# A hybrid encoder layer: one block pair fewer by seven products, and the activation sums of the down-projection on VectorE

## The chip, the cores and the metric

The kernel runs on one core of one Trainium2 chip. The metric is the device time of one execution in microseconds, as the median of several runs; lower is better. Engines are named as in the profile: PE (TensorE, matmul), ACT (ScalarE), DVE (VectorE), POOL (GpSimd), SP (SyncE, which here only issues DMAs). ACT issues some DMAs too; each engine works through its queue in order.

## The reference

One layer on x (512 tokens x 1024 channels), all in float32: four gated token mixers with a merge, cross-attention, and a gated MLP. The change concerns the MLP alone:

```python
hf = _rms_norm(x, norm_ffn_pre[l])                                  # (512, 1024)
u = _dwconv_causal(hf @ w_up[l], ffn_dw[l]) + ffn_dw_b[l]           # (512, 2 * 2816), width 3
u_g, u_v = jnp.split(u, 2, axis=-1)
yff = (jax.nn.silu(u_g) * u_v) @ w_down[l]                          # (512, 1024)
x = x + _rms_norm(yff, norm_ffn_post[l])
```

## The kernel before

**Products.** A float32 product is made of three passes on PE (`mm3`, matmuls on L244): each operand is split into a high part, a cast by ACT, and a low part, a subtraction by DVE. Weights are split on L201 (ACT) and L202 (DVE), operands of the down-projection on L1653 and L1654. High and low weights have rings of four buffers each (`wh`, `wl`), raw weights a ring of two (`wr`). The activations of the MLP lie in two tiles, `hth` and `htl`.

**The up-projection** runs over 22 blocks j of 128 hidden channels, each with a gate half (j, 0) and a value half (j, 1). A plain product `plain(j, i)` is 24 matmuls of 512 columns. `done` evacuates it: a bias step on ACT (L1678), two taps on DVE (L624), and after the second half a Silu on ACT (L1681) and a product on DVE (L1683) into the tile `qa` of the block's pair, `ns.quart[j // 2]`. So there are eleven pairs, q = 0 to 10.

`seven(j)` makes both halves of a block at once from seven quarter products of 12 matmuls of 256 columns instead of eight. For it POOL forms four sums of the block's weights (L1756 to L1760), and sums of the activations lie in `tokh` and `tokl`; DVE adds up the parts in PSUM, and ACT copies parts to `mu` (L1782, L1788, L1790) that PE waits for before it accumulates on. The blocks 5, 7, ... 19 go by seven, each interleaved with the plain block after it; 0 to 4 and 21 are plain.

**The down-projection** goes by seven products over the eleven pairs in two phases of two jobs per pair. It needs two kinds of sums:

- *of the weights* (`Sums`): for each pair ACT issues two loads of `w_down` into `wp` (L568), four additions follow (L572 to L575, on DVE for the pairs 0 to 2 and 10, on POOL otherwise), and ACT issues two stores to `sums` in DRAM (L579). They are spread over the up-projection. The down jobs load them back as `dw` (L591, issued by SP).
- *of the activations* (`down_sums`): for each pair three additions of 128 x 256 on POOL, L1665 and L1666 into a place `pairs`, L1667 into the pair's `qa`. The places are in the tile `z7` for the pairs 0 and 1, which the last block by seven gives up, and in `tokh` and `tokl` for the others.

Each pair's activations and their sums are then split into a quarter of `hth` and `htl`, which the last up product still reads (the first pair goes to `wr` buffers). One more POOL addition per pair (L1888) follows for the second phase.

**Buffers in common.** The tags `dw0` to `dw3` serve `wp` (the first two), the raw weights `wq` of the blocks by seven (the other two) and the down weights `dw` (all four).

**The order** on each engine is set by a scheduler that places the traced instructions by its own times. `tc.issue_after` only queues an instruction behind another on the same engine. The jobs are run by `run_blocks`, which fetches weights three jobs ahead.

## Time and profile before

| | |
|---|---|
| median of 3 runs | 1049.4 us (1047.03 to 1051.22) |
| profiled execution | 1049.59 us |
| its span | 1047.7 us |
| granted clock of PE, mean | 0.993 |
| PE busy | 1024.8 us (98%) |
| DVE busy | 855.1 us (82%) |
| ACT busy | 534.0 us (51%) |
| POOL busy | 290.7 us (28%) |
| HBM traffic over the span | 161 GB/s |

The profiled execution lies within the runs' spread; the 1.9 us between its time and its span are outside the program's instructions. Times in the lines of the profile are microseconds from the start of the span. A timeline line gives start, length, engine, line, operation, output and inputs, shapes, the number of instructions merged, and in brackets how long the engine was idle before and what it waited for; ACTq and SPq are DMA issues. A line of the list of waits gives who waited for whom, the total, the number of times and the longest. A line of the table of stretches gives the stretch, its length, for PE, PEld (weight load), DVE, ACT and POOL the busy time and in brackets the number of instructions, then the granted clock of PE, the DMA engines' share and GB/s. The chain of waits lists, in order of time, the work that the end of the program hung on. A busy PE is not PE at its peak: two matmuls of 512 columns follow each other at 0.2275 us.

### The profile page before, as it was taken

The page shows a single profiled execution, that of the slowest core. Times are in us where ns is not written, and L with a number is a line of the kernel's source. Part 1 is how long each engine was busy: PE and PEld are TensorE (multiplying, and loading weights), DVE is VectorE, ACT ScalarE, POOL GpSimd, SP SyncE. Part 2 cuts the span into 40 slices and gives each one's busy share as a digit, 9 for nine tenths or more (in the row PEclk, how much of TensorE's full clock was granted, in tenths as well). Part 3 has the DMA queues.
Part 4 walks back from the last instruction along what each step waited for, and adds up shares of the span by engine and source line. Part 5 has one row for each costly group of instructions (what it writes and reads, how often), then busy time and mean ns, then how long its engine had stood idle before and what let it go on. Part 6 is the DMA issues. An engine that isn't in the chain of part 4 may idle for free.

```text
span 1047.7 us, 15194 instructions
## 1 busy us (share of the span) xinstructions
PE 1024.8 (98%) x5477; PEld 883.3 (84%) x5477; DVE 855.1 (82%) x1290; ACT 534.0 (51%) x893; POOL 290.7 (28%) x303
## 2 busy tenths in 40 slices
PE   9999999999999999999999999999999999969997
PEld 7888888888888988888888899898789899848885
DVE  7899998677788668878677898769887887879786
ACT  5322222376565465765535666554455454545662
POOL 4001000100020224332000030166077547696001
PEclk9999999999999999999999999999999999989999
DMA  7954333334444356676368743054776566536562
GB/s 252 307 171 106 101 101 101 91 91 127 135 116 114 94 136 180 173 195 172 122 206 266 222 141 121 22 181 127 235 241 200 182 220 204 180 120 221 195 209 90
DMA packets 194129, 169.41 MB, mean 162 GB/s; under 512 B 25295, under 2 KB 165692, under 8 KB 194053
## 3 DMA queue, kind: packets, MB, share of 16 engines
q1 hardware_dynamic: 185011, 136.69, 44.1%
q10 hardware_dynamic: 6482, 23.21, 6.0%
q0 software_dynamic: 2560, 8.54, 2.6%
q8 instruction: 43, 0.70, 0.3%
q14 instruction: 33, 0.27, 0.1%
HBM read 142.18 MB, written 26.23 MB: 161 GB/s over the span
## 4 chain that ended last, share of the span: by engine, by line
PE 87%; DMA 4%; DVE 4%; POOL 2%; issue 2%; ACT 2%; ACTq 0%; SPq 0%; POOLq 0%; DVEq 0%
PE ps_mm L244 38%; PE ps_av L244 23%; PE ps_tr L244 14%; PE ps_sc L244 9%; PE ps_tr L250 1%; DMA dw<-sums 1%; POOL pairs L1666 1%; DMA sums<-wp 1%; DVE wl L202 1%; DMA ptl<-turned 1%; DMA e<-in_w_in 1%; POOL pairs L1665 1%; PE ps_mm L462 1%; DMA wp<-in_w_down 1%; PE ps_av L462 1%
## 5 line engine op out<-in xcount | busy, mean ns | idle before, releaser
L201 ACT CAST wh<-wr 128x1024 fp32r<-128x1024 f32 (+1 forms) x124 | 129.4, 1046 | 185.6 <-PE ps_mm L244 67.7
L202 DVE TENSOR_TENSOR wl<-wr,wh 128x1024 fp32r<-128x1024 f32 (+1 forms) x124 | 161.9, 1307 | 37.5 <-ACT wh L201 36.9
L244 PE MATMUL ps_mm<-htl,wh 128*128 128x512 f32 (+1 forms) x472 | 173.5, 376 | 0.0
L244 PE MATMUL ps_mm<-hth,wh 128*128 128x512 f32 (+1 forms) x472 | 173.5, 376 | 0.0
L244 PE MATMUL ps_mm<-hth,wl 128*128 128x512 f32 (+1 forms) x472 | 173.2, 375 | 0.0
L244 PEld LDWEIGHTS ps_mm<-hth,wl 128*128 128x128 f32 x472 | 87.0, 188 | 15.8
L244 PEld LDWEIGHTS ps_mm<-hth,wh 128*128 128x128 f32 x472 | 87.0, 188 | 15.3 <-ACT hth L164 0.3
L244 PEld LDWEIGHTS ps_mm<-htl,wh 128*128 128x128 f32 x472 | 87.0, 188 | 15.3
L244 PE MATMUL ps_av<-htl,wh 128*128 128x512 f32 (+1 forms) x264 | 97.7, 370 | 0.0
L244 PE MATMUL ps_av<-hth,wh 128*128 128x512 f32 (+1 forms) x264 | 97.6, 370 | 0.0
L244 PE MATMUL ps_av<-hth,wl 128*128 128x512 f32 (+1 forms) x264 | 97.6, 370 | 0.0
L697 DVE SCALAR_TENSOR_TENSOR y<-y,par,y 128x508 f32<-128x508 f32 (+29 forms) x120 | 82.5, 726 | 0.1
L244 PEld LDWEIGHTS ps_av<-htl,wh 128*128 128x128 f32 x264 | 49.6, 188 | 8.2
L244 PEld LDWEIGHTS ps_av<-hth,wl 128*128 128x128 f32 x264 | 49.6, 188 | 8.0
L244 PEld LDWEIGHTS ps_av<-hth,wh 128*128 128x128 f32 x264 | 49.7, 188 | 7.9
L1654 DVE TENSOR_TENSOR wl<-dw,wh 128x1024 fp32r<-128x1024 f32 x32 | 44.0, 1377 | 7.7 <-ACT wh L1653 7.5
L1653 ACT CAST wh<-dw 128x1024 fp32r<-128x1024 f32 x32 | 33.5, 1050 | 17.8 <-PE ps_tr L244 5.7
L244 PE MATMUL ps_tr<-htl,wh 128*128 128x512 f32 (+1 forms) x112 | 40.6, 363 | 0.0
L244 PE MATMUL ps_tr<-hth,wh 128*128 128x512 f32 (+1 forms) x112 | 40.6, 363 | 0.0
L244 PE MATMUL ps_tr<-hth,wl 128*128 128x512 f32 (+1 forms) x112 | 40.4, 360 | 0.0
L1124 POOL TENSOR_SCALAR fbias<-ck,cq 128x128 f32<-128x128 f32 (+3 forms) x32 | 21.3, 670 | 66.2 <-DVE st L1130 61.1
L811 POOL MEMSET qk<- 64x512 f32 x16 | 8.5, 532 | 90.5 <-PE ps_sc L244 31.8
(558 smaller groups left out, 2770.8 us busy)
## 6 DMA issues: line engine op xcount, KB each, us to landing
wr<-in_w_in SPq DMA_DIRECT2D x38, 512.0 KB
wr<-in_w_gate SPq DMA_DIRECT2D x32, 512.0 KB
wr<-in_w_up SPq DMA_DIRECT2D x28, 512.0 KB
wp<-in_w_down ACTq DMA_DIRECT2D x22, 512.0 KB
sums<-wp ACTq DMA_DIRECT2D x22, 512.0 KB
dw<-sums SPq DMA_DIRECT2D x44, 256.0 KB
wr<-in_w_branch SPq DMA_DIRECT2D x16, 512.0 KB
wq<-in_w_up SPq DMA_DIRECT2D x16, 512.0 KB
```

The source lines that it names most:

```text
L201: last_weights[:] = [order(A.copy(hi, raw[:, :n])).ins, low.tensor_tensor(lo, raw[:, :n], hi.bitcast(F32), ALU.subtract).ins]
L202: low.tensor_tensor(lo, raw[:, :n], hi.bitcast(F32), ALU.subtract).ins]
L244: steps_of[:] = [PE.matmul(ps, lhs, rhs, start=start, stop=stop, skip_group_check=again).ins]
L250: turns.append(PE.transpose(ps, x, ident[:n, :n]).ins)
L462: keep(PE.matmul(banks[c][:, :S // 2], w[p == 1][:, k, c * P:(c + 1) * P], ht[p == 2][:, i * 4 + k, :S // 2], start=(i, p, k) == (0, 0, 0) ...
L697: ins = V.scalar_tensor_tensor(dst[:, s:], src[:, :S - s], pc("conv_dw", k * 4 + j), dst[:, s:], ALU.mult, ALU.add)
L811: G.memset(qk[rows[1 - c], 4 + c].bitcast(F32), 0.0)
L1124: G.tensor_scalar(bias[:, :w], ck[j][:, :w], -1.0, cq[:, qt, head:head + 1], ALU.mult, ALU.add)
L1653: A.copy(hi, x)
L1654: V.tensor_tensor(lo, x, hi.bitcast(F32), ALU.subtract)
L1665: G.tensor_tensor(t[:, 0], x[:, 1], x[:, 3], ALU.add)
L1666: G.tensor_tensor(t[:, 1], x[:, 0], x[:, 1], ALU.subtract)
```

## The change

- The blocks 5 to 17 go by seven (seven pairs of blocks); 19, 20 and 21 are plain.
- `down_sums` runs on DVE instead of POOL. The sums of the pairs 0 and 1 get a place in the tag `qa10` from the start and are traced in the rounds of the blocks 9 and 13; those of the pairs 2 to 5 with the last plain products; those of 6 to 10 inside the down-projection's first phase, two pairs ahead. Places for the pairs 2 to 10 are taken once the last block by seven is through, two blocks of plain products earlier than before. The last pair's `qa` moves into `tokl`.
- The weight sums of the pairs 9 and 10 move to the plain products: store 9 and load 10 with (19, 0), additions of 10 with (20, 0), store 10 with (20, 1).
- The additions of the pair 2 are traced after the first part of block 5 (before: with (4, 1)), its store after the first half of (6, 1).

```diff
@@ -1647,24 +1647,25 @@
 
     def token_split(i):
         hi, lo = ns.tok
-        split_to(hi[:, i], lo[:, i], ns.quart[i - 4])
+        A.copy(hi[:, i], ns.quart[i - 4])
+        V.tensor_tensor(lo[:, i], ns.quart[i - 4], hi.bitcast(F32)[:, i], ALU.subtract)
 
     def split_to(hi, lo, x):
         A.copy(hi, x)
         V.tensor_tensor(lo, x, hi.bitcast(F32), ALU.subtract)
 
-    def down_places(*places):
-        for tag, n in places:
-            x = ns.fp.tile([P, 2 * n, S // 2], F32, tag=tag, name="pairs")
-            ns.pair_sums += [x[:, 2 * i:2 * i + 2] for i in range(n)]
+    def down_places(tag, n, more=0):
+        x = ns.fp.tile([P, 2 * n + more, S // 2], F32, tag=tag, name="pairs")
+        ns.pair_sums += [x[:, 2 * i:2 * i + 2] for i in range(n)]
+        return x[:, 2 * n:]
 
     def down_sums(*pairs):
 
         for q in pairs:
             x, t = ns.quart[q], ns.pair_sums[q]
-            G.tensor_tensor(t[:, 0], x[:, 1], x[:, 3], ALU.add)
-            G.tensor_tensor(t[:, 1], x[:, 0], x[:, 1], ALU.subtract)
-            G.tensor_tensor(x[:, 1], t[:, 0], x[:, 0], ALU.subtract)
+            V.tensor_tensor(t[:, 0], x[:, 1], x[:, 3], ALU.add)
+            V.tensor_tensor(t[:, 1], x[:, 0], x[:, 1], ALU.subtract)
+            V.tensor_tensor(x[:, 1], t[:, 0], x[:, 0], ALU.subtract)
 
     def up_jobs():
         st, held = {}, []
@@ -1736,13 +1737,6 @@
                         sums_step(f, x, "taps")
             return now
 
-        yield plain(2, 0, steps(("store", 0)))
-        yield plain(2, 1, steps(("load", 1), ("split", 1)))
-        yield plain(3, 0, steps(("add", 1), ("split", 0)))
-        yield plain(3, 1, steps(("store", 1), ("split", 2)))
-        yield plain(4, 0, steps(("load", 2), ("split", 3)))
-        yield plain(4, 1, steps(("add", 2)))
-
         def seven(j):
 
             z = SimpleNamespace()
@@ -1807,8 +1801,20 @@
                     (lambda: split_weights(z.v, [P, NK, P], shift=HALF_SHIFT), None, body_c),
                     (lambda: split_weights(z.t, [P, 4, P], shift=HALF_SHIFT), None, body_d), then(end))
 
-        for q, j in enumerate(range(5, NF - 2, 2)):
-            load_a, body_a, b, c, d, e = seven(j)
+        def early_places():
+            ns.pair_sums = []
+            down_places(f"qa{NF // 2 - 1}", 2)
+
+        pairs = {j: seven(j) for j in range(5, NF - 4, 2)}
+        yield plain(2, 0, steps(("store", 0)))
+        yield plain(2, 1, steps(("load", 1), ("split", 1)))
+        yield plain(3, 0, steps(("add", 1), ("split", 0)))
+        yield plain(3, 1, steps(("store", 1), ("split", 2)))
+        yield plain(4, 0, steps(("load", 2), ("split", 3)))
+        yield plain(4, 1, early_places)
+
+        for q, j in enumerate(pairs, 2):
+            load_a, body_a, b, c, d, e = pairs[j]
             a = load_a, None, body_a
             tail = {}
 
@@ -1823,30 +1829,36 @@
                     mm3(tail["ps"], hi[:, k], lo[:, k], ns.hf[0][:, k], ns.hf[1][:, k], False, k == NK - 1)
                 done(j, 1, tail["ps"])
 
-            end = j + 4 > NF
             yield a
+            if q == 2:
+                yield then(lambda: add_sums(2, V, "taps"))
             yield plain(j + 1, 0)
-            yield then(lambda q=q: sums_step("store", q + 2, "first"))
+            if q > 2:
+                yield then(lambda q=q: sums_step("store", q, "first"))
             yield b
-            if end:
-                yield then(lambda q=q: sums_step("load", q + 3, "taps"))
             yield (*block(j + 1, 1), first_half)
-            if end:
-                ns.pair_sums = []
-                yield then(lambda: (down_places(("z7", 2)), down_sums(0, 1)))
-            else:
-                yield then(lambda q=q: sums_step("load", q + 3, "taps"))
+            if q == 2:
+                yield then(lambda q=q: sums_step("store", q, "first"))
+            yield then(lambda q=q: sums_step("load", q + 1, "taps"))
             yield c
+            if q in (4, 6):
+                yield then(lambda q=q: down_sums(q // 2 - 2))
             yield d
             yield then(lambda j=j, f=second_half: f(j + 1))
-            if end:
-                yield then(lambda q=q: add_sums(q + 3, V, "taps"))
             yield e
-            if not end:
-                yield then(lambda q=q: ns.sums.add(q + 3, G))
-        yield then(lambda: down_places(("tokh", 8), ("tokl", 1)))
-        yield plain(NF - 1, 0, lambda: (sums_step("store", NF // 2 - 1, "taps"), down_sums(2, 3)))
-        yield plain(NF - 1, 1, lambda: down_sums(*range(4, NF // 2)))
+            yield then(lambda q=q: ns.sums.add(q + 1, G))
+        last = NF // 2 - 1
+        def late_places():
+            down_places("tokh", 8)
+            ns.quart[-1] = down_places("tokl", 1, 4)
+
+        yield then(late_places)
+        yield plain(NF - 3, 0, lambda: (sums_step("store", last - 1, "taps"), sums_step("load", last, "taps")))
+        yield plain(NF - 3, 1, lambda: down_sums(2))
+        yield plain(NF - 2, 0, lambda: add_sums(last, V, "taps"))
+        yield plain(NF - 2, 1, lambda: (sums_step("store", last, "taps"), down_sums(3)))
+        yield plain(NF - 1, 0, lambda: down_sums(4))
+        yield plain(NF - 1, 1, lambda: down_sums(5))
 
     def down_jobs():
         pairs, hold, half = NF // 2, 4, S
@@ -1883,6 +1895,8 @@
                 for i, part in enumerate((x[:, :2], ns.pair_sums[q])):
                     cut = slice(i * S, i * S + S)
                     split_to(hi[:, cut], lo[:, cut], part.rearrange("p a b -> p (a b)"))
+                if 6 <= q + 2 < pairs:
+                    down_sums(q + 2)
                 for i in range(max(q - 2, 0), q - 1 if q < pairs - 1 else pairs):
                     z = ns.quart[i]
                     G.tensor_tensor(z[:, 1], z[:, 2], z[:, 1], ALU.subtract)
```

The scheduler places it all anew. Three places of the new order follow, with the numbers of the buffers; lines of the code behind the additions stand one further down than before.

ACT around the end of the last up product (its bias step reads `ps_av_8998` before, `ps_av_8944` now). Before:

```order
L1678 ACTIVATE c_8979<-ps_av_8998,par2_406 128x512
L1653 CAST hth_8944<-pairs_8939 128x512
L1653 CAST htl_8945<-pairs_8939 128x512
L579 DMA sums_6875<-wp_8817 128x1024
L1653 CAST hth_8944<-qa_6862 128x512
L1681 ACTIVATE c_8979<-c_8979 128x512
L1653 CAST htl_8945<-qa_6863 128x512
L1653 CAST wh_9084<-dw_8991 128x1024
L1653 CAST htl_8945<-qa_6864 128x512
L1653 CAST wh_8994<-dw_8871 128x1024
L1653 CAST wh_9057<-dw_8941 128x1024
L1653 CAST wh_9108<-dw_9049 128x1024
```

Now:

```order
L1654 CAST htl_8896<-qa_6863 128x512
L1654 CAST htl_8896<-pairs_8717 128x512
L1654 CAST htl_8896<-qa_6864 128x512
L1654 CAST htl_8896<-pairs_8717 128x512
L1654 CAST hth_8895<-qa_6861 128x512
L1654 CAST hth_8895<-pairs_7249 128x512
L1679 ACTIVATE c_8930<-ps_av_8944,par2_406 128x512
L1654 CAST hth_8895<-qa_6862 128x512
L1654 CAST hth_8895<-pairs_8717 128x512
L1654 CAST wh_9012<-dw_8937 128x1024
L1654 CAST wh_8940<-dw_8844 128x1024
L1654 CAST wh_8985<-dw_8892 128x1024
```

Before, the casts of the down-projection's operands and of its weights (`wh<-dw`) follow the bias step mixed, with a store between; now six casts, among them those of the pair 1 (`qa_6861`, `pairs_7249`), stand ahead of the bias step, and the weight casts behind two more.

The sums of the activations: POOL before, while PE runs the last plain product.

```order
L1665 TENSOR_TENSOR pairs_8939<-qa_6868 128x256
L1666 TENSOR_TENSOR pairs_8939<-qa_6868 128x256
L1666 TENSOR_TENSOR pairs_8939<-qa_6869 128x256
L1667 TENSOR_TENSOR qa_6862<-pairs_8939,qa_6862 128x256
L1888 TENSOR_TENSOR qa_6860<-qa_6860 128x256
L1667 TENSOR_TENSOR qa_6863<-pairs_8939,qa_6863 128x256
L1667 TENSOR_TENSOR qa_6864<-pairs_8939,qa_6864 128x256
L1667 TENSOR_TENSOR qa_6865<-pairs_8939,qa_6865 128x256
L1666 TENSOR_TENSOR pairs_8940<-qa_6870 128x256
L1667 TENSOR_TENSOR qa_6866<-pairs_8939,qa_6866 128x256
L1667 TENSOR_TENSOR qa_6867<-pairs_8939,qa_6867 128x256
L1665 TENSOR_TENSOR pairs_8939<-qa_6869 128x256
```

Now on DVE, from the point at which PE has let `tokh` go; `wl` are the low weights of the plain products.

```order
L1667 TENSOR_TENSOR pairs_8717<-qa_6866 128x256
L1666 TENSOR_TENSOR pairs_8717<-qa_6867 128x256
L1667 TENSOR_TENSOR pairs_8717<-qa_6867 128x256
L202 TENSOR_TENSOR wl_8659<-wr_8656,wh_8658 128x1024
L624 SCALAR_TENSOR_TENSOR c_8578<-ps_av_8620,par0_398,c_8578 128x511
L1667 TENSOR_TENSOR pairs_8717<-qa_6868 128x256
L624 SCALAR_TENSOR_TENSOR c_8675<-ps_tr0_8521,par0_398,c_8675 128x510
L1668 TENSOR_TENSOR qa_6862<-pairs_8717,qa_6862 128x256
L1668 TENSOR_TENSOR qa_6863<-pairs_8717,qa_6863 128x256
L1668 TENSOR_TENSOR qa_6864<-pairs_8717,qa_6864 128x256
L1668 TENSOR_TENSOR qa_6865<-pairs_8717,qa_6865 128x256
L1668 TENSOR_TENSOR qa_6866<-pairs_8717,qa_6866 128x256
```

What was POOL's row of sums now stands in DVE's queue between weight splits (L202) and taps (L624). In PE's queue the first four matmuls of the down-projection now stand ahead of (21, 0).

DVE early in the up-projection, around the weight sums of pair 1 (`wp_7080`, `wp_7079`), before:

```order
L624 SCALAR_TENSOR_TENSOR c_7116<-ps_mm_7091,par0_398,c_7116 128x510
L202 TENSOR_TENSOR wl_7131<-wq_7126,wh_7130 128x1024
L624 SCALAR_TENSOR_TENSOR c_7116<-ps_mm_7091,par0_398,c_7116 128x511
L572 TENSOR_TENSOR wp_7080<-wp_7080,wp_7079 128x512
L573 TENSOR_TENSOR wp_7079<-wp_7079 128x512
L574 TENSOR_TENSOR wp_7079<-wp_7080,wp_7079 128x512
L202 TENSOR_TENSOR wl_7177<-wr_7174,wh_7176 128x1024
L575 TENSOR_TENSOR wp_7080<-wp_7080,wp_7079 128x512
L624 SCALAR_TENSOR_TENSOR c_7116<-ps_av_7140,par0_398,c_7116 128x510
L624 SCALAR_TENSOR_TENSOR c_7116<-ps_av_7140,par0_398,c_7116 128x511
L1683 TENSOR_TENSOR qa_6861<-c_7116 128x512
```

Now:

```order
L1666 TENSOR_TENSOR pairs_7249<-qa_6860 128x256
L1667 TENSOR_TENSOR pairs_7249<-qa_6860 128x256
L202 TENSOR_TENSOR wl_7131<-wq_7126,wh_7130 128x1024
L1667 TENSOR_TENSOR pairs_7249<-qa_6861 128x256
L624 SCALAR_TENSOR_TENSOR c_7116<-ps_mm_7091,par0_398,c_7116 128x511
L1668 TENSOR_TENSOR qa_6860<-pairs_7249,qa_6860 128x256
L572 TENSOR_TENSOR wp_7080<-wp_7080,wp_7079 128x512
L202 TENSOR_TENSOR wl_7177<-wr_7174,wh_7176 128x1024
L573 TENSOR_TENSOR wp_7079<-wp_7079 128x512
L624 SCALAR_TENSOR_TENSOR c_7116<-ps_av_7140,par0_398,c_7116 128x510
L574 TENSOR_TENSOR wp_7079<-wp_7080,wp_7079 128x512
L624 SCALAR_TENSOR_TENSOR c_7116<-ps_av_7140,par0_398,c_7116 128x511
```

The sums of the pairs 0 and 1 stand ahead of and among the weight sums L572 to L574, and a weight split has moved ahead of L573.

## The prediction

> **What bounds the kernel now.** The first view is the page's line of engines, the second the table of stretches.
>
> ```profile
> PE 1024.8 (98%) x5477; PEld 883.3 (84%) x5477; DVE 855.1 (82%) x1290; ACT 534.0 (51%) x893; POOL 290.7 (28%) x303
> 850.00:900.00 50.00, 50.00 (x315) 45.16 (x314) 42.62 (x47) 25.43 (x36) 32.73 (x21) 1.00 0.62 194
> 900.00:950.00 50.00, 39.95 (x198) 33.70 (x198) 40.30 (x46) 24.51 (x36) 40.73 (x36) 0.90 0.45 158
> ```
>
> PE is busy for 98% of the span, so a change gains only where PE stands still or by giving it less to do. In the stretch 850 to 900 us it is never idle. In 900 to 950 it is busy 39.95 of 50 us and its granted clock is 0.90: here, around the passage from the up products to the down products, lies the one large hole that the change can reach. The list of waits says who ended PE's idle time from 600 us on, and who ended that of the engine in front of it.
>
> ```profile
> PE ps_sc L244 <- ACT wh L1653: 10.0, 1, 10.0
> PE ps_tr L244 <- ACT mu L1782: 1.5, 1, 1.5
> PE ps_tr L244 <- ACT mu L1788: 1.4, 1, 1.4
> ACT hth L1653 <- POOL qa L1667: 7.3, 1, 7.3
> ```
>
> One wait of 10.0 us, for a cast of ACT; ACT itself waited 7.3 us for one of POOL's activation sums (L1667). The timeline puts them in order, PE first, then ACT, then POOL.
>
> ```profile
> 923.25 0.39 PE L244 MATMUL ps_sc<-wh,wr 128*128 128x512 f32 x1
> 927.91 0.39 PE L244 MATMUL ps_mm<-wh,wr 128*128 128x512 f32 x1
> 938.35 1.22 PE L244 MATMUL ps_sc<-wh,hth 128*128 128x512 f32 x2 [10.05 <-ACT wh L1653]
> ```
> ```profile
> 923.28 0.62 ACT L1653 CAST htl<-pairs 128x512 fp32r<-128x512 f32 x1 [1.23 <-PE ps_av L244]
> 923.80 0.61 ACT L1653 CAST hth<-qa 128x512 fp32r<-128x512 f32 x1
> 924.85 0.77 ACT L1678 ACTIVATE c<-ps_av,par 128x512 f32<-128x512 f32 x1
> 925.52 0.61 ACT L1653 CAST hth<-pairs 128x512 fp32r<-128x512 f32 x1
> 926.03 0.62 ACT L1653 CAST htl<-pairs 128x512 fp32r<-128x512 f32 x1
> 933.90 0.62 ACT L1653 CAST hth<-qa 128x512 fp32r<-128x512 f32 x1 [7.25 <-POOL qa L1667]
> 937.26 1.99 ACT L1653 CAST wh<-dw 128x1024 fp32r<-128x1024 f32 x2
> ```
> ```profile
> 894.87 2.37 POOL L574 TENSOR_TENSOR wp<-wp 128x512 f32<-128x512 f32 x1
> 914.40 0.75 POOL L1665 TENSOR_TENSOR pairs<-qa 128x256 f32<-128x256 f32 x1 [9.27 <-PE ps_tr L244]
> 929.75 0.71 POOL L1665 TENSOR_TENSOR pairs<-qa 128x256 f32<-128x256 f32 x1
> 934.51 2.99 POOL L1667 TENSOR_TENSOR qa<-pairs,qa 128x256 f32<-128x256 f32 x3
> ```
>
> The last up product ends at 923.25, where the first down matmul starts (call that moment E). The down product's first weights last PE until 928.3. The next ones, of q=1, are behind ACT's cast hth<-qa at 933.90, which waits for POOL: POOL can begin its sums of q=2 and later only at 914.40, when PE has let the tile tokh go, and works through them in one row until after 934. That row ends last; ACT's casts and PE's restart at 938.35 follow from it.
>
> The hole costs more than its 10.05 us, as the granted clock (the column behind the five engines) shows.
>
> ```profile
> 930.00:931.00 1.00, 0.00 (x0) 0.00 (x0) 0.00 (x0) 0.00 (x0) 1.00 (x2) 1.00 0.90 303
> 931.00:932.00 1.00, 0.00 (x0) 0.00 (x0) 0.00 (x0) 0.00 (x0) 1.00 (x3) 0.56 0.22 84
> 940.00:941.00 1.00, 1.00 (x3) 0.79 (x3) 1.00 (x2) 0.00 (x0) 1.00 (x2) 0.50 0.63 178
> 941.00:942.00 1.00, 1.00 (x5) 0.79 (x4) 1.00 (x1) 0.36 (x1) 1.00 (x1) 0.82 0.90 330
> ```
>
> The clock is whole until 931, 0.56 on average in the next us and half from then until the us that averages 0.82. By those shares it fell at 931.1, 2.8 us after PE's last matmul ended, and came back at 941.4, 3.0 us after the restart: 3.0 us at half speed lose 1.5 us. The DMA share of 0.22 in 931 to 932 shows that the loads had landed by then; they are not what PE waited for.
>
> **The change, part by part.** *One pair fewer by seven products.* A plain product is 24 matmuls of 512 columns, a quarter product 12 of 256:
>
> ```profile
> 852.91 5.46 PE ps_mm L244 x24
> 858.38 1.42 PE ps_tr L244 x12
> ```
>
> Block 19 costs 2 x 5.46 = 10.92 us where it cost 7 x 1.41 = 9.87: PE gets 1.05 us more, all of it on the path, since PE never rests there. The block's four weight sums on POOL and its three PSUM additions on VectorE go; POOL was not waited for there, so that gives nothing.
>
> *The sums move from POOL to VectorE.* 33 additions of 128x256. VectorE's price for that shape in SBUF stands in no row; from below it follows from these:
>
> ```profile
> 925.41 0.73 DVE L624 SCALAR_TENSOR_TENSOR c<-ps_mm,par,c 128x511 f32<-128x511 f32 x1
> 926.07 0.67 DVE L1654 TENSOR_TENSOR hth<-qa,hth 128x512 fp32r<-128x512 f32 x1
> 917.43 1.21 DVE L1654 TENSOR_TENSOR wl<-dw,wh 128x1024 fp32r<-128x1024 f32 x1
> 934.55 1.23 DVE L1654 TENSOR_TENSOR hth<-qa,hth 128x512 fp32r<-128x512 f32 x1 [5.35 <-ACT hth L1653]
> ```
>
> 1024 columns take 1.21 us and 512 take 0.67, so 256 take about 0.40, of which about 0.07 overlaps the next: 0.34 each (estimate from these rows). From above the bound is 1.23 us, what even 512 columns took beside a busy POOL. I take 0.34, since POOL is nearly empty there in the new order, and keep the other end for a rival. 25 sums stand in VectorE's queue between tokh's release and E, so 8.5 us, in a stretch of 33 us in which PE runs six plain products. The removed quarter products free some of it: they need 3.5 weight splits for block 19, two plain products need 2, and the split is 1.21. Walking the new queues with the old durations, VectorE is ready with each split 3 to 8 us before PE wants it. The tightest is that of (20, 0): tokh is free at about 892.8, twelve sums take 4.1; ACT's cast waits in its queue behind a store that wants POOL's L574 (894.87 + 2.37) and ends at 898.4, the split at 899.6; PE wants it at 902.6. And VectorE ends the last thing that ACT wants before E (the taps of the product (21, 0)) 1.9 us before E. So the sums cost PE nothing as long as these margins hold; behind them in VectorE's queue stand the splits, for which PE waits.
>
> *What is late next.* With POOL's row gone, ACT's queue decides. From E it issues six casts of 512 columns, the bias step of the last product, two more such casts, then the weight casts of q=2, of q=1 and of q=1 again. The rows at 923.28, 923.80, 924.85 and 925.52 give a pitch of 0.525 us per cast and 0.67 for the bias step; the two casts in the row at 937.26 give at most 1.0 each, two neighbours give 0.95:
>
> ```profile
> 910.31 1.05 ACT L1653 CAST wh<-dw 128x1024 fp32r<-128x1024 f32 x1 [2.17 <-PE ps_sc L244]
> 911.26 1.04 ACT L201 CAST wh<-wr 128x1024 fp32r<-128x1024 f32 x1
> ```
>
> 6 x 0.525 + 0.67 + 2 x 0.525 + 2 x 0.95 = 6.8 us after E the first weights of q=1 are ready. PE has 17 matmuls of 0.2275 (5.46 / 24) left at E, 3.9 us; four of the old 21 were put ahead of the last two products. So PE still waits, 6.8 - 3.9 = 2.9 us rather than 10.05. VectorE makes the low halves behind ACT, at 0.60 us per 512 columns, 1.14 per 1024 and 0.66 per taps step (the rows above less 0.07): those of q=1 are ready at 9.1 and 10.9 us. PE asks for the first 2.5 us after its restart, at 9.3, so it waits no more.
>
> The DMAs behind it hang on the last store of weight sums.
>
> ```profile
> 924.91 0.33 ACTq L579 DMA_DIRECT2D sums<-wp  x1
> ```
>
> It leaves ACT at about 923.1 in the new queues, when its fourth sum on VectorE ends. After the row above the loads were through 6.5 us later (the window at 931); that makes 929.6, and ACT reaches those weights at E + 5.8, which is 931.0 with E at 925.2 (923.25 + 1.05 + the four early matmuls, 0.91). They just fit.
>
> *Four POOL additions (qa<-qa) after E* stay, and run beside VectorE's splits. The row at 934.55 shows what that costs VectorE: 1.23 rather than 0.67, 0.56 each. At nothing they are hidden, at 4 x 0.56 the low half of q=1 comes at 11.3 rather than 9.1 and PE, wanting it at 9.3, stands 2.0 us more. I take 0.7, nearer the lower end, because the first two fall where VectorE still waits for ACT's casts.
>
> *The early pairs and the later store.* The scheduler draws the sums of q=0 and q=1 forward, into VectorE's queue ahead of the sums of w_down that ACT's store waits for. There ACT blocks in its queue and the copies `mu` behind it hold PE (the waits of 1.5 and 1.4 us above).
>
> ```profile
> 742.13 0.69 DVE L574 TENSOR_TENSOR wp<-wp 128x512 f32<-128x512 f32 x1
> 742.86 2.07 ACTq L579 DMA_DIRECT2D sums<-wp  x2
> 745.86 0.34 ACTq L568 DMA_DIRECT2D wp<-in_w_down  x1
> 749.88 0.34 ACTq L568 DMA_DIRECT2D wp<-in_w_down  x1
> 752.46 0.36 ACT L1782 COPY mu<-ps_tr 128x256 f32<-128x256 f32 x1
> ```
>
> The store follows L574 by 0.1 us, the first load its store by 3.0 us, the second load the second store by about 5, and mu comes after a Silu, a cast and a bias step. Four of the six sums, a split and a taps step now stand ahead of L574 and put it at 744.9, 2.1 us later. But the block ends with the DMA: VectorE's split that lets the next load of weights go comes about 1 us earlier, so that load no longer shares the DMA engines with the second store, which then needs about 3 us, as the first did, rather than 5, and the second load is issued at 749.9 again (estimate). Bounds: 0 (absorbed) and +2.1 (passed on whole). I take 0. That add_sums(2) and its store stand later in the text changes nothing in ACT's queue there: the store still stands just ahead of the second mu.
>
> *Sum,* against the profiled execution's 1049.59 us (the median of the three runs, 1049.4, is the same within their spread).
>
> ```profile
> 948.90 1.36 PE ps_mm L244 x6
> ```
>
> Out: the wait 10.05 and the slow restart; from 938.35 to the row above PE did 39 matmuls, 8.87 us of work in 10.55, so 1.68. In: 1.05 for block 19, 2.9 for the new wait, 0.7 beside POOL, 0 early. 1049.59 - 11.73 + 4.65 = 1042.5.
>
> [...]
>
> [...]
>
> **The rivals.** *ACT's queue leaves a short wait* (the forecast, 1042.5): chance 0.55, with 1041 to 1044.
>
> *No wait is left.* If ACT's casts for q=1 slip ahead, PE goes through: 1049.59 - 11.73 + 1.05 = 1038.9. For it speaks that ACT is mostly idle before E; against it that the casts write hth and htl, which PE reads until E. Chance 0.12.
>
> *The gain is half given back.* The early delay of 2.1 us passes on, the new wait passes the point at which the clock falls (another 1.5), and VectorE lies 1 us behind: 1042.5 + 4.6 = 1047.1. [...] For it: the wait is within 0.1 us of the fall seen above, and ACT's block near 745 has no slack. Chance 0.23, 1044.2 to 1048.
>
> *VectorE becomes the bound, slower.* Place: the last three blocks' products. If the 25 sums cost 1.23 each, VectorE gets 25 x 0.89 = 22 us more; its margin before E is 1.9, and ACT's store and casts behind it wait, so PE stands about 20 us longer: 1063. It decides from 1.9 us onward, and is slower than now once VectorE is 1.9 + 7.1 = 9.0 us behind, at 0.70 us a sum. Against it: VectorE's operations were slowed only beside POOL, and POOL has four additions of weights there. Chance 0.06.
>
> *The sums weren't it.* If the loads of q=1 held PE all the same, its wait shrinks to the landing at 931.5 and the casts behind it: a gain of about 3 us, 1046 to 1050. Against it: ACT's 7.3 us on POOL in the list of waits, which ended 2.4 us after that landing. Chance 0.04.
>
> **How the numbers follow.** About 0.5% (5.2 us) is what a measurement of this kernel can tell from no change. Faster by more, below 1044.2: the forecast and the case without a wait, 0.67. Within: the half-given-back case and the last, 0.27. Slower: 0.06. The range runs from 1038.9, no wait at all, to 1047.6, which takes in most of the half-given-back case.
>
> **What would show it.** Right: no POOL sums left before the down products; a PE wait on an ACT weight cast some 4 us after E, 2 to 4 us long; the clock at full or half for 3 us at most; 25 sums of about 0.4 us on VectorE between tokh's release and E; the two waits on mu near 752 and 760 within 1 us of the old ones. Wrong: waits of PE on VectorE's splits in the products (19, 0) to (21, 1); a store of the last sums issued after E; a wait on mu of 3 us or more; a new hole in the down products, where I see no cause for one.

## The result, and the profile after

| | before | changed |
|---|---|---|
| median (lowest to highest), first measurement | 1049.91 us (1047.03 to 1051.22, 4 runs) | 1044.24 us (1043.63 to 1045.63, 4 runs) |
| ratio, with its 95% interval | | 0.9952 (0.9928 to 0.9975) |
| the same, measured again later | 1049.17 us (1047.51 to 1050.65, 15 runs) | 1045.62 us (1043.81 to 1046.26, 6 runs) |
| ratio | | 0.9965 (0.9952 to 0.9977) |
| profiled execution; its span; mean clock | 1049.59; 1047.7; 0.993 | 1044.80; 1043.0; 0.996 |

The change makes the kernel 3.6 to 5.7 us faster. The forecast was 1042.5, with 1038.9 to 1047.6 as its range.

Three views answer to those shown of before: the line of engines, two stretches, and PE's waits in the whole run from 600 us on.

```profile
PE 1027.3 (98%) x5441; PEld 883.7 (85%) x5441; DVE 856.6 (82%) x1318; ACT 531.7 (51%) x888; POOL 241.7 (23%) x266
```
```profile
850.00:900.00 50.00, 50.00 (x296) 44.38 (x296) 42.09 (x52) 23.37 (x33) 22.69 (x14) 1.00 0.61 202
900.00:950.00 50.00, 44.95 (x185) 36.17 (x184) 46.01 (x67) 25.29 (x35) 9.55 (x7) 0.93 0.49 164
```
```profile
PE ps_sc L244 <- ACT wh L1654: 4.7, 1, 4.7
PE ps_tr L244 <- ACT mu L1782: 1.4, 1, 1.4
PE ps_tr L244 <- ACT mu L1776: 0.9, 1, 0.9
PE ps_sc L244 <- DVE wl L202: 0.3, 1, 0.3
```

POOL is nearly out of the stretch 900 to 950 (9.55 us busy, 40.73 before), VectorE fills it (46.01 of 50). The hole of 10.05 us is one of 4.73, again on a weight cast of ACT; PE is busy 44.95 us there instead of 39.95, though at a mean clock of 0.93. The timeline around the end of the last up product (E, now 924.07), PE first, then ACT, then VectorE:

```profile
924.07 0.39 PE L244 MATMUL ps_sc<-wl,wr 128*128 128x512 f32 x1
927.79 0.40 PE L244 MATMUL ps_mm<-wh,wr 128*128 128x512 f32 x1
932.92 1.22 PE L244 MATMUL ps_sc<-wh,hth 128*128 128x512 f32 x2 [4.73 <-ACT wh L1654]
```
```profile
925.52 0.63 ACT L1682 ACTIVATE c<-c 128x512 f32<-128x512 f32 x1 [5.01 <-DVE c L624]
926.06 0.60 ACT L1654 CAST htl<-qa 128x512 fp32r<-128x512 f32 x1
930.87 2.94 ACT L1654 CAST wh<-dw 128x1024 fp32r<-128x1024 f32 x3
924.69 0.74 DVE L624 SCALAR_TENSOR_TENSOR c<-ps_mm,par,c 128x511 f32<-128x511 f32 x1
```

ACT's row is what the prediction walked: six casts, the bias step, two casts, two weight casts, and it takes 6.8 us (926.06 to the end of the second of the three casts in the last ACT row, about 932.9). But it starts 2.0 us after E, not at E. ACT stood 5.01 us at a Silu that waits for VectorE's taps of (21, 0), and these ended at 925.43, after E. The chain of waits says why; its rows are start, length, engine, line:

```profile
892.55 1.50 DVE pairs L1667
...
899.60 1.15 DVE wl L202
...
900.76 5.21 DMA wr<-in_w_up
...
906.04 1.06 ACT wh L201
...
924.77 0.67 DVE c L624
...
931.82 1.05 ACT wh L1654
...
932.92 1.22 PE ps_sc L244 x2
```

From 888 to 925 the end of the program hangs on VectorE and, for 6 us, on a load of raw weights, which starts when VectorE's split frees the buffer, and its cast. The dear ones of the 25 sums stand near the row's start. The timeline of VectorE, and one row of POOL beside it:

```profile
892.55 1.50 DVE L1667 TENSOR_TENSOR pairs<-qa 128x256 f32<-128x256 f32 x1
893.97 1.51 DVE L1666 TENSOR_TENSOR pairs<-qa 128x256 f32<-128x256 f32 x1
895.40 1.51 DVE L1667 TENSOR_TENSOR pairs<-qa 128x256 f32<-128x256 f32 x1
896.84 0.41 DVE L1666 TENSOR_TENSOR pairs<-qa 128x256 f32<-128x256 f32 x1
893.85 1.35 POOL L574 TENSOR_TENSOR wp<-wp 128x512 f32<-128x512 f32 x1
```

POOL makes the weight sums of pair 9 from 890.4 to 896.6. Three of VectorE's sums beside them take 1.43 each from start to start (the one before them 0.78); when POOL is through they follow at 0.335, the 0.34 of the prediction. The three alone are 3.3 us over, and from there to 925 VectorE stands idle only once, for 0.34 us.

### The profile page after: what moved, and what is told of

It reads as the page before. It is cut to its first block, busy times and chain, and to the rows that moved or that the text cites. A ratio compares the mean times of both kernels' runs of the same rounds, so it can differ in the third digit from the quotient of the medians.

```text
span 1043.0 us, 15098 instructions
## 1 busy us (share of the span) xinstructions
PE 1027.3 (98%) x5441; PEld 883.7 (85%) x5441; DVE 856.6 (82%) x1318; ACT 531.7 (51%) x888; POOL 241.7 (23%) x266
## 4 chain that ended last, share of the span: by engine, by line
PE 94%; DVE 4%; issue 1%; ACT 1%; DMA 0%; POOL 0%; POOLq 0%; DVEq 0%; ACTq 0%
PE ps_mm L244 41%; PE ps_av L244 24%; PE ps_tr L244 14%; PE ps_sc L244 11%; PE ps_tr L250 1%; DVE c L624 1%; DVE wl L202 1%; PE ps_mm L462 1%; PE ps_av L462 1%; DMA wr<-in_w_up 0%; DVE pairs L1667 0%; DVE pairs L1666 0%; PE ps_mm L403 0%; PE ps_sc L408 0%; DVE qa L1684 0%
## 5 line engine op out<-in xcount | busy, mean ns | idle before, releaser
L201 ACT CAST wh<-wr 128x1024 fp32r<-128x1024 f32 (+1 forms) x126 | 131.5, 1047 | 196.3 <-PE ps_mm L244 70.3
L202 DVE TENSOR_TENSOR wl<-wr,wh 128x1024 fp32r<-128x1024 f32 (+1 forms) x126 | 164.5, 1306 | 37.6 <-ACT wh L201 36.9
L244 PE MATMUL ps_mm<-hth,wh 128*128 128x512 f32 (+1 forms) x480 | 176.6, 376 | 0.0
L244 PE MATMUL ps_mm<-htl,wh 128*128 128x512 f32 (+1 forms) x480 | 176.6, 376 | 0.0
L244 PE MATMUL ps_mm<-hth,wl 128*128 128x512 f32 (+1 forms) x480 | 176.3, 376 | 0.0
L244 PE MATMUL ps_av<-htl,wh 128*128 128x512 f32 (+1 forms) x272 | 100.8, 371 | 0.0
L244 PE MATMUL ps_av<-hth,wh 128*128 128x512 f32 (+1 forms) x272 | 100.7, 370 | 0.0
L244 PE MATMUL ps_av<-hth,wl 128*128 128x512 f32 (+1 forms) x272 | 100.7, 370 | 0.0
L1655 DVE TENSOR_TENSOR wl<-dw,wh 128x1024 fp32r<-128x1024 f32 x32 | 41.0, 1283 | 8.4 <-ACT wh L1654 8.3
L857 DVE STREAM_TRANSPOSE e<-e 128x128 f32<-128x128 f32 (+3 forms) x46 | 32.5, 728 | 0.3
```

The source lines that it names most:

```text
L201: last_weights[:] = [order(A.copy(hi, raw[:, :n])).ins, low.tensor_tensor(lo, raw[:, :n], hi.bitcast(F32), ALU.subtract).ins]
L202: low.tensor_tensor(lo, raw[:, :n], hi.bitcast(F32), ALU.subtract).ins]
L244: steps_of[:] = [PE.matmul(ps, lhs, rhs, start=start, stop=stop, skip_group_check=again).ins]
L857: V.transpose(dst, src.rearrange("p (t j b) -> p b t j", b=4, j=32))
L1655: V.tensor_tensor(lo, x, hi.bitcast(F32), ALU.subtract)
```

## The experiments

Two theories stood against each other. A: VectorE's lateness and the length of ACT's row set PE's restart. B: the loads of the down weights behind the last store of weight sums set it. Each time is the median of its runs, with its ratio to the kernel before on the same chip.

### Which half of the change brings the gain: the engine or the order

The kernel before with its sums on VectorE:

```diff
-            G.tensor_tensor(t[:, 0], x[:, 1], x[:, 3], ALU.add)      # and the two below
+            V.tensor_tensor(t[:, 0], x[:, 1], x[:, 3], ALU.add)
```

> The kernel before with the activation sums on VectorE and nothing else changed. Before: 1049.9 us, the changed kernel 1044.2. Theory A (VectorE is the bound around the passage, and its last taps start ACT's row of casts): 27 of the 33 sums now fall on VectorE after tokh's release at 914.4, 9 us before the last up product ends; 27 x 0.34 = 9.2 us do not fit there beside the taps, so the row of casts and the last store come late. PE's hole shrinks from 10.05 by less than half, to 5 to 9 us: 1045 to 1049. Theory B (the loads of the down weights behind the last store of weight sums set the restart): the third of pair 10's weight sums moves behind some 20 activation sums, the store goes out about 5 us later, and the hole is as long as before or longer: 1049 to 1054. If the engine alone were the whole of the gain: 1044, hole 4 to 5 us.

Measured: 1057.31 us, ratio 1.0075 (1.0062 to 1.0089): slower, and by more than either theory gave. PE's waits:

```profile
PE ps_mm L244 <- DVE c L624: 8.5, 1, 8.5
PE ps_sc L244 <- ACT wh L1653: 4.1, 1, 4.1
PE ps_tr L244 <- DVE c L624: 2.9, 1, 2.9
```

The hole is not shorter but split in three, 15.5 us together. Three quarters of it is PE waiting for VectorE's taps themselves, which free the PSUM banks: VectorE became the bound, the mechanism of the prediction's slower rival. With the engine alone the change would have lost 8 us.

The changed kernel with its sums back on POOL (the same edit backwards):

> The changed kernel with all activation sums back on POOL: the new order of blocks and places alone. Theory A: VectorE loses 25 x 0.34 = 8.5 us of sums and the 3.3 us by which three of them ran long beside POOL; it gains what POOL's row costs it. At the 0.53 us by which a VectorE step of 512 columns ran long beside one POOL addition after the restart (1.21 rather than 0.68), 22 POOL sums cost 11.7 us, and the time stays at 1043 to 1046. If POOL's sums cost VectorE nothing, VectorE is on time, ACT starts its casts when the last up product ends and the hole falls to 1 to 3 us: 1039 to 1042; then the engine was not needed for the gain. Theory B: the store goes out when VectorE has made pair 10's weight sums, earlier by what VectorE is ahead; hole 2 to 4 us.

Measured: 1045.33 us, ratio 0.9963 (0.9949 to 0.9976), which can't be told from the changed kernel's 0.9952 and 0.9965. One wait of PE, ACT's Silu and the two weight casts behind it, and two kinds of VectorE steps beside POOL's row:

```profile
PE ps_sc L244 <- ACT hth L1654: 5.0, 1, 5.0
```
```profile
928.71 0.63 ACT L1682 ACTIVATE c<-c 128x512 f32<-128x512 f32 x1 [4.56 <-DVE c L624]
930.95 1.04 ACT L1654 CAST wh<-dw 128x1024 fp32r<-128x1024 f32 x1 [1.61 <-DMA dw<-sums]
932.22 1.04 ACT L1654 CAST wh<-dw 128x1024 fp32r<-128x1024 f32 x1 [0.23 <-DMA dw<-sums]
918.32 1.19 DVE L572 TENSOR_TENSOR wp<-wp 128x512 f32<-128x512 f32 x1
924.55 1.52 DVE L624 SCALAR_TENSOR_TENSOR c<-ps_av,par,c 128x510 f32<-128x510 f32 x2
922.36 1.18 POOL L1666 TENSOR_TENSOR pairs<-qa 128x256 f32<-128x256 f32 x1
```

VectorE is late here too, although it has no sums: its additions of 512 columns take 1.1 to 1.2 where they took 0.68, its taps (two in 1.52) what they took in the changed kernel (two in 1.53 at 888.53). But the Silu that waited 4.56 us for it is not what ends PE's wait. Behind it ACT stood another 1.61 and 0.23 us for loads of down weights, and the cast of activations that PE waits for stands behind those two weight casts: here the load is the bound, as B says. So the equal times are made of different parts; this profile also has a wait of 1.90 us on `mu` at 753.79, behind which PE's matmuls of 256 columns follow each other at 0.21 us instead of 0.12 for 3.4 us (754.49 to 757.89).

Measured by the time, then, the new order, with either engine, brings the whole measurable gain; that VectorE makes the sums is worth nothing measurable there. The order includes block 19 by plain products: with it PE lets `tokh` go at about 891 instead of 914, which leaves the sums 33 us before E rather than 9.

### ACT's row or the loads

The weight sums of pair 10 one product earlier, so that the last stores leave earlier:

```diff
-        yield plain(NF - 3, 1, lambda: down_sums(2))
-        yield plain(NF - 2, 0, lambda: add_sums(last, V, "taps"))
+        yield plain(NF - 3, 1, lambda: (add_sums(last, V, "taps"), down_sums(2)))
+        yield plain(NF - 2, 0)
```

> The changed kernel with the weight sums of pair 10 one product earlier (with (19, 1) rather than (20, 0)); all else stands in the same order on PE, SP and POOL. The store goes out 1 to 2 us earlier, the first load of q = 1 lands that much earlier. Theory A: VectorE's last taps before ACT's row of casts end where they did (925.4), the casts keep their places, PE restarts at 932.9 within 0.4 us: 1043.8 to 1044.6. Theory B: PE restarts 1 to 2 us earlier, and the time falls to 1042 to 1043.3.

Measured: 1045.07 us, ratio 0.9958 (0.9946 to 0.9971): no change. The wait is still there, 4.46 us:

```profile
933.71 1.22 PE L244 MATMUL ps_sc<-wh,hth 128*128 128x512 f32 x2 [4.46 <-ACT wh L1654]
```

The four early down matmuls start 1.06 us later in this profile (913.18 rather than 912.12). Against them the first of the two last stores (922.75, before 922.94) is 1.25 us earlier than in the changed kernel, and PE's restart only 0.3 us. In this profile ACT's row starts 0.80 us later than in the changed kernel (926.86) and PE restarts 0.79 later: the restart keeps to the row and not to the store. B alone is refuted for the changed kernel.

ACT's casts of q = 2 to 4 behind the first weight cast of q = 1:

```diff
             if job and n + 1 < 2 * len(order):
-                activations(*order[(n + 1) // 2])
+                with tc.issue_after(parts["cast"]) if n in (3, 5, 7) else ExitStack():
+                    activations(*order[(n + 1) // 2])
...
+            if n == 2:
+                parts["cast"] = ns.cast          # the weight cast of q = 1, set in split_to
```

> The changed kernel with ACT's six casts of the activations of q = 2 to 4 put behind the first weight cast of q = 1. Theory A: from the row's start at 926.1 ACT has two casts (1.05), the bias step (0.67) and two weight casts (1.9), so q = 1's first weights are ready at 929.7 rather than 932.9, and PE, out of work at 928.2, waits 1.5 to 2 us rather than 4.7. That is 3 us less, and with so short a wait the clock may stay up, 2.8 us more: 1038.4 to 1041.4, unless PE meets a new wait for the casts put back. Theory B: the first load of q = 1 lands at 931, the weight cast waits for it, PE restarts at 932 to 932.9: 1043 to 1044.3.

Measured: 1042.36 us (1040.74 to 1042.78), ratio 0.9927 (0.9912 to 0.9941). PE's rows, and ACT's weight cast:

```profile
930.05 0.47 PE L244 MATMUL ps_av<-wh,wr 128*128 128x512 f32 x1 [1.39 <-DVE c L624]
931.28 0.84 PE L244 MATMUL ps_sc<-wh,hth 128*128 128x512 f32 x2 [0.30 <-ACT wh L1654]
930.17 1.05 ACT L1654 CAST wh<-dw 128x1024 fp32r<-128x1024 f32 x1 [0.91 <-DMA dw<-sums]
```

The long wait is gone: ACT's row made it, as A says. The time lies between the two forecasts. What is left is 1.39 us for a PSUM bank that VectorE's taps of (21, 1) free, and 0.30 for the weight cast, which itself waited 0.91 us for its load. So B's bound lies close behind A's: the cast ends at 931.2, which is 2.2 us before the changed kernel's restart when the 0.46 us by which this profile runs later are taken off. The clock fell all the same (0.50 from 931.74 to 935.15, see the last section), which A's range had not allowed for.

### Is VectorE's lateness worth anything by itself

The changed kernel again, beside the next three:

> The changed kernel unchanged, on the same chip as the runs beside it, so that they can be compared directly. All theories: 1043.6 to 1045.6, with one wait of PE on the weight cast of q = 1 of 4.5 to 5 us.

Measured: 1045.62 us, ratio 0.9965; the profiled execution, 1045.65 us, has a mean clock of 0.996, the same as in the changed kernel's first profile.

Without POOL's additions for pair 9 (this kernel leaves these sums out and serves only for timing):

```diff
-            yield then(lambda q=q: ns.sums.add(q + 1, G))
+            if q < 8:
+                yield then(lambda q=q: ns.sums.add(q + 1, G))
```

> The changed kernel without POOL's four additions of the weight sums of pair 9 (their part of the down-projection then uses unsummed weights); the order after them is the same but for a few places. In the changed kernel VectorE's sums that run beside these four took 1.50 us each, 4.3 for three of them with the fourth's start, where the ones behind them follow at 0.335. Theory A (VectorE's lateness sets the start of ACT's casts): VectorE is 3 us earlier from 897 on, the taps of (21, 0) end before the last up product does, ACT starts its casts 1.5 to 2 us earlier relative to it, and PE waits 2.7 to 3.2 us instead of 4.7: 1.5 to 2 us less than the changed kernel, 1042 to 1043. Rival (the sums that ran long beside POOL lie beside other waits, and the loads or ACT set the start): PE's wait stays within 0.4 us, the time within 0.5.

Measured: 1044.58 us (1042.94 to 1046.38), ratio 0.9959 (0.9945 to 0.9972), a wait of 4.58 us. The wait is the rival's, but not for its reason; the time lies 1.0 us below the changed kernel's, between the two forecasts, and here the clock was halved for 3.41 us rather than 6.82.

```profile
885.15 6.53 DMA wp<-in_w_down
...
892.14 0.79 ACT c L1679
...
896.28 0.33 DVE pairs L1666
```

The sums do follow at 0.34 (the chain's last row), so the price of 1.43 was POOL's doing. But with nothing to wait for, the store of pair 9 moved ahead of a bias step in ACT's queue and held ACT until the load of pair 9 had landed at 891.8; VectorE's row of sums started about 4 us later than in the changed kernel (896.28, before 891.77, less 0.55 for the later profile), and the taps of (21, 0) ended when they did there (925.83, less 0.55). So VectorE caught up the 4 us on the way, about the price that the sums had paid beside POOL; what that price is worth at the end of the program this run doesn't tell.

The sums of the pairs 6 to 10 behind the last taps:

```diff
                 if 6 <= q + 2 < pairs:
-                    down_sums(q + 2)
+                    with tc.issue_after(ns.taps):          # the taps of (21, 1)
+                        down_sums(q + 2)
```

> The changed kernel with the sums of the pairs 6 to 10 held behind the taps of the last up product on VectorE: 13 sums, 4.4 us, leave the stretch before the end of the up products. Theory A: VectorE is on time, ACT starts its row of casts when the last up product ends; the row has the same length (one weight cast moves ahead of it), so PE restarts 6.5 to 7 us after that end rather than 8.8 and waits 2.6 to 3.1 us: 1.5 to 2.2 us less than the changed kernel, 1042 to 1043, if the sums cost nothing where they now stand; among the splits for which PE waits they may cost up to 4.4 us. Rival (VectorE's lateness is harmless): the same time as the changed kernel or up to 4.4 us more.

Measured: 1045.53 us, ratio 0.9960 (0.9944 to 0.9976), but with runs from 1040.53 to 1046.81. The median is the rival's; the profile is of the fastest run, which beats even A's range, so this run decides nothing. In that profile VectorE's taps of (21, 0) end 2.3 us before E, no wait of PE in the passage is longer than 0.64 us, and ACT's row has a weight cast at its head that waited 3.56 us for its load:

```profile
924.43 1.05 ACT L1654 CAST wh<-dw 128x1024 fp32r<-128x1024 f32 x1 [3.56 <-DMA dw<-sums]
```

Three edits together (pair 10's weight sums earlier, the casts put back, the sums held):

> All three edits on the changed kernel: sums of the pairs 6 to 10 behind the last taps, pair 10's weight sums one product earlier, and casts of q = 2 to 4 behind the first weight cast of q = 1. Theory A: VectorE is on time, the store of the last weight sums is issued about 3 us earlier so that q = 1's first weights are cast before the last up product ends; five casts of activations (2.6 us) stay behind it, less than PE's 3.9 us of work, so the passage has no wait over 0.5 us and the clock stays up: 1038.5 to 1040.5, some 4 to 5 us below the changed kernel. If a new wait of PE on VectorE's splits takes its place (13 sums now among them): 1040.5 to 1043.

Measured: 1046.14 us, ratio 0.9974 (0.9963 to 0.9984): a miss, slower than the changed kernel and 3.8 us slower than the casts put back alone. PE's restart, ACT's row up to its first cast of activations, and the store in the chain of waits:

```profile
932.62 0.76 PE L244 MATMUL ps_sc<-wh,hth 128*128 128x512 f32 x1 [4.97 <-ACT hth L1654]
924.15 0.63 ACT L1682 ACTIVATE c<-c 128x512 f32<-128x512 f32 x1 [2.59 <-DVE c L624]
927.27 1.05 ACT L1654 CAST wh<-dw 128x1024 fp32r<-128x1024 f32 x1 [2.49 <-DMA dw<-sums]
929.45 1.04 ACT L1654 CAST wh<-dw 128x1024 fp32r<-128x1024 f32 x1 [1.13 <-DMA dw<-sums]
930.40 0.61 ACT L1654 CAST htl<-qa 128x512 fp32r<-128x512 f32 x1
```
```profile
920.40 5.56 DMA sums<-wp
```

VectorE is earlier here: the Silu is through at 924.8, 1.4 us sooner than in the changed kernel. But two weight casts now stand ahead of the casts of activations, and ACT stands 2.49 and 1.13 us for their loads, with five casts behind it that wait for nothing. The load waits for a store that takes 5.56 us beside other loads, and then takes 3.0 itself. Here B's bound holds. A load that lands a little later would do the same to the kernel with only the sums held, which has such a cast at the head of its row. That this makes the spread of its runs is not shown: only the fastest was profiled.

### Taking both bounds away

The first load of q = 1 hangs on the store only because it goes into the buffer that the store reads. The tile `z7` is free by then:

```diff
-                raw = dw_tile("dw")
+                raw = dw_tile("dw") if len(raws) != 2 else ns.fp.tile([P, D], F32, tag="z7", name="dw")
```

> The changed kernel with one load moved: the first weights of q = 1 go into the tile z7, which the last block by seven has given up and nothing uses there, rather than into the buffer that holds pair 10's weight sums until their store is through. The load then hangs on no store, and its cast stands ahead of the end of the last up product (E) in ACT's queue; the Silu of the last block, which waits for VectorE's late taps, now stands behind the six casts. Theory A (ACT's row, started late by VectorE, made the wait) and B (the load did) both say that the wait of 4.7 us goes; six casts (3.15 us) end before PE's 3.9 us of work. What is left: the PSUM bank of (21, 1), which VectorE's taps free at about E + 5 (a wait of 1 to 1.5), and the second weights of q = 1, whose store is now issued behind the bias step, at 928: landing at about 934, cast at 935, up to 2 us late. With the clock up: 1039.5 to 1042.5, against 1044 to 1045.6 for the changed kernel. If the time does not fall below 1043.5, the wait only changed its owner.

Measured: 1040.39 us (1039.81 to 1041.38), ratio 0.9915 (0.9901 to 0.9929). The waits that PE has left in the passage, and ACT's first cast behind E:

```profile
933.33 0.73 PE L244 MATMUL ps_mm<-wh,hth 128*128 128x512 f32 x2 [0.36 <-ACT wh L1654]
934.68 0.50 PE L244 MATMUL ps_av<-wh,wr 128*128 128x512 f32 x1 [0.38 <-DVE c L624]
926.08 0.62 ACT L1654 CAST htl<-qa 128x512 fp32r<-128x512 f32 x1 [3.02 <-PE ps_av L244]
```

The cast starts when PE lets `htl` go (its 3.02 us of idle time ended by PE), though VectorE's taps of (21, 0) end at 928.5, 2.4 us after E (926.11): once no Silu stands in front of the casts, VectorE's lateness no longer holds them. With pair 10's sums one product earlier as well:

> As the kernel with the load in z7, and pair 10's weight sums one product earlier: both stores are issued before the end of the last up product, so the second weights of q = 1 land by about 931 and are cast when PE asks for them (933). Left is the wait for the PSUM bank of (21, 1), 1 to 1.5 us. 1038.5 to 1041.5; at least 1 us below the kernel with the load in z7 if its second weights were late there, the same if not.

Measured: 1039.72 us (1039.15 to 1041.06), ratio 0.9909 (0.9894 to 0.9924); two waits of 0.49 and 0.65 us are left between 905 and 950. The clock stays whole around the end of the up products in both profiles (1.00 over 900 to 950). The last edit gains nothing that can be told from the run before. Both beat the kernel before and the changed one; the intervals of this one and of the changed kernel don't overlap.

## Why the prediction was right, and where its terms were off

**The hole.** The 10.05 us went, as forecast, and ACT's queue decided what came next, in the order and with the 6.8 us that were walked. The new wait was put at 2.9 and measured 4.73. The step that failed is the margin of VectorE ("VectorE ends the last thing that ACT wants before E (the taps of the product (21, 0)) 1.9 us before E"). They ended 1.4 us after it, 3.3 later than forecast, so ACT's row began 2.0 us after E, and the wait grew by 1.8. The margin rested on 0.34 us for each of 25 sums: 21 kept to it, one took 0.78, and three took 1.43 beside POOL's additions for pair 9, 3.3 us too much. That these three made the margin go is a sum that fits; no run took their price away and left the rest in place. The upper bound of 1.23 was named, and set aside with "POOL has four additions of weights there". Four were enough.

The load was not what held ACT. In the run with the casts put back it had landed at 930.17, which is 929.7 with the 0.46 us taken off, and with VectorE on time ACT would have reached that cast at E + 5.8, 929.9. The prediction's "They just fit" held, by 0.2 us, though the load landed 1.2 us later after E than forecast.

**The clock.** The second wrong term is the clock, for which the sum of 1042.5 has nothing: the slow restart of 1.68 us went out of it, and one of 2.88 came back (half speed from the restart at 932.92 to 938.69, 5.77 us). No run shows that a wait of 2.9 us leaves the clock whole, as that sum takes it: it fell around waits of 1.39 and 0.30 us (the casts put back) as well, and stayed whole only where no wait of the passage was longer than 0.65.

**The small terms.** Block 19: from the second wait on `mu` to E it is 163.24 us before and 165.75 after; less the four early matmuls (0.91) and the wait of 0.32 at 912.12, that is 1.28 for the forecast 1.05. Beside the four POOL additions after E two of VectorE's splits took 1.21 and 1.22 instead of 0.68, but PE waited for none of them: 0, forecast 0.7. The early pairs: the waits on `mu` are 0.94 and 1.39, before 1.46 and 1.39, so 0.5 gained, forecast 0.

**The sum.** 1049.59 - 10.05 + 4.73 - 1.68 + 2.88 + 1.28 + 0.32 - 0.5 = 1046.6. The profile measured 1044.8; 1.3 of the difference was there before the MLP began (the same matmul at 642.54 before and 641.25 after), in code that the change doesn't touch, and 0.5 is unexplained. By its own terms the forecast was 4 us too low (wait 1.8, clock 2.9, the small wait 0.3, block 19 0.2, less 0.7 and 0.5); the 1.8 that have nothing to do with them hid a part. That the median of 1044.24 lies only 1.7 us from the forecast is to that extent luck; the first step, that POOL's row made the hole and that it would go, is not.

**The rivals.** What came true is the rival "half given back" in two of its three parts, the clock and VectorE behind by 1 to 2 us, and not the forecast's case; the repeated measurement (1045.6) lies in that rival's 1044.2 to 1048. "VectorE becomes the bound" is half true: the chain runs over VectorE for 37 us, but PE stood only about 2 us longer for it. That the engine change is what brings the gain was taken for granted, and the runs don't bear it out: the order with POOL's sums reaches the same time, and the engine without the order loses.

## What to carry to other kernels

When a slow engine's row of work is the bound, ask first when that row may begin. Here the new order, which lets that buffer go 23 us earlier, was worth about 4 us with either engine, and the other engine without it cost 8. Then look at what the late queue really holds: a cast that waits for a load, or a Silu that waits for taps, should not stand ahead of work that waits for nothing, and a load should not hang on a store only because both use one buffer.

## What the hardware showed

**The clock moved on a grid.** In stretches of 0.1 us the clock fell and came back at 931.11 and 941.35 before, 931.87 and 938.69 after. It fell once more near the end of both profiles, at 1043.75 and 1041.09, 112.64 and 109.22 us behind its first fall: 33 and 32 times 3.413. Around the end of the up products it stayed at half for 10.24 us before and for 6.82 in the changed kernel and in the one with pair 10's weight sums earlier, and for 3.41 with the changed kernel's sums on POOL, with ACT's casts put back, without POOL's additions for pair 9, and with the three edits together: whole multiples of 3.41. In the kernel before with its sums on VectorE the mean over 900 to 950 is 0.78, so about 22 us of these 50 were at half; with the sums held and in the two kernels with `z7` it is 1.00. The stretches of that grid, of before, of the changed kernel, and of the one with ACT's casts put back:

```profile
927.70:931.11 3.41, 0.60 (x3) 0.16 (x1) 1.50 (x3) 0.00 (x0) 3.41 (x4) 1.00 0.81 276
937.94:941.35 3.41, 3.00 (x7) 2.42 (x8) 3.41 (x3) 1.30 (x2) 3.41 (x4) 0.50 0.29 89
```
```profile
928.46:931.87 3.41, 0.00 (x0) 0.00 (x0) 3.41 (x5) 3.41 (x7) 2.09 (x3) 1.00 0.51 181
931.87:935.28 3.41, 2.36 (x6) 1.88 (x7) 3.41 (x6) 1.94 (x3) 1.29 (x2) 0.50 0.00 0
935.28:938.69 3.41, 3.41 (x10) 2.64 (x9) 3.38 (x5) 1.04 (x1) 0.00 (x0) 0.50 0.67 213
```
```profile
928.33:931.74 3.41, 1.72 (x7) 0.90 (x6) 3.38 (x6) 2.50 (x5) 0.72 (x1) 1.00 0.76 257
```

In these views the clock fell at the end of a stretch in which PE was busy 0.60, 0.00 or 1.72 us of 3.41, and rose at the end of one with 3.00 or 3.41; 2.36 did not raise it. PE's busy time alone does not settle it: in the kernel without POOL's additions for pair 9 a stretch with 1.53 us (927.21 to 930.63; the last matmul ended at 928.74) left the clock whole, and it fell only at 934.04, after one with 0.72; what decides there stays open. So a wait costs its length and, where the clock falls, up to 1.7 us more (half of 3.41, an estimate) for each stretch at half speed. Where the grid lay differed between executions (a fall at 931.11 before, 931.87 in the changed kernel, 931.74 with ACT's casts put back, 934.04 without POOL's additions for pair 9), and a wait of 4.58 us cost one such stretch in the last of these, one of 4.73 two in the changed kernel. The prediction measured its wait of 2.9 us against the 2.8 us from the last matmul to the fall, and put the rise 3.0 us after the restart. Neither length stayed: the fall came 3.7 us after the last matmul in the changed kernel and 5.3 without POOL's additions for pair 9, the rise 5.8 and 4.1 us after the restart.

**VectorE's additions took longer beside POOL's.** A sum of 256 columns beside POOL's additions of 512 took 1.43, about POOL's 1.35 and not its own 0.34, and without those additions the sums followed at 0.34; taps, which read PSUM, kept their time beside POOL (two in 1.52). In the rows here a short step beside long ones paid most: 1.1 us for each of those sums, about 0.5 for an addition of 512 columns beside POOL's 256.
